# Expert gates of a PEER layer: two tokens interleaved instead of four, and the sum of both parts kept in the order of the activations

## The chip, the cores and the metric

The kernel runs on one core of one Trainium2 chip. The metric is the device time of one execution in microseconds (us): the median of several runs, here three. One further execution was recorded by the hardware profiler, and all rows below are from it. TensorE (PE) multiplies a moving operand by weights that it loads first (PEld), VectorE (DVE) and ScalarE (ACT) work elementwise, SyncE (SP) issues the transfers.

## The reference, cut to what matters

The program is two transformer blocks behind each other on 256 tokens of width 1024. The change lies in the last layer only, a PEER layer: each token picks, in each of 8 heads, 16 of 128 x 128 experts, with a softmax gate for each.

```python
q = (xt @ wq).reshape(T, PEER_HEADS, 2, PEER_HALF)
s = jnp.einsum('thpd,hpnd->thpn', q, subkeys).astype(jnp.float32)
top_s, top_i = lax.top_k(s, PEER_TOPK)
...
gates = jax.nn.softmax(best_s, axis=-1)
...
hdn = jax.nn.gelu(jnp.einsum('cd,chkd->chk', xc, uc).astype(jnp.float32), approximate=False) * gc
return jnp.einsum('chk,chkd->cd', hdn.astype(vc.dtype), vc)
```

An expert's number is 128 i1 + i2. A token has 128 slots (8 heads x 16), each with one i1, one i2 and one gate.

## The kernel before, in words

The layer is computed densely. For every i1 (a row r of 128) one 512 KB tile of `pu` and one of `pv` is loaded. In the first pass (the u pass) the tile of `pu` is split into two f32 parts (`whi` by ACT on L124, `wlo` by DVE on L125) and multiplied with all 256 tokens: 24 matmuls of 256 columns into `pu` (`mm3`, L184 to L186). ACT takes the gelu into `H[i2, r, token]` (L1629). In the second pass (the v pass) `H` of two rows is split (`hs`, ACT on L1728, DVE on L1729) and multiplied with the split tile of `pv`: 12 matmuls of 512 columns per row into the four accumulators `pout`. Between the two, each value of `H` has to be multiplied by its gate.

The gates are made by `gates(g, t0)`, once for each half g of the i1 (64 each) and each group of G = 8 tokens: 64 calls. On the partitions stand the token's 128 slots. DVE compares each slot's i2 with the numbers 0 to 127 (`b`, L1662) and each slot's i1 with the 64 numbers of the half (`e`, L1664), in f16, and multiplies `e` by both f16 parts of the gate (`a`, two calls of L1667). For each token one matmul (L1673) with `b` as weights and `a` as moving operand (2 parts x 64 columns) sums over the slots, so `pw[i2, token, part, i1]` holds the gates of the token twice over, as two parts. ACT copies part 1 out of PSUM to `s` (L1675), DVE adds part 0 (L1676) and multiplies the sum into `H` (L1677).

In memory `b`, `e` and `a` hold four tokens side by side (the last dimension is 4, in blocks n), so that a matmul that picks one token reads its columns 4 elements of f16 apart, which is 8 bytes. `iob` is the list of numbers, each four times. `s` is in the order token, i1, while `H` is in the order i1, token; so L1677 reads `s` with neighbouring elements 64 f32, 256 bytes, apart.

The order is written out by hand: `work()` is a generator, and after every two rows `step()` takes as many pieces from it as its budget allows and as their due rows ask for (`GCOST` and `BUDGET` are constants of the program that the change does not touch). The engines run their instructions in this order. Buffers: `b`, `a` and `pw` have two each, `e` and `s` one.

Of the kernel before, what the change touches and what calls it, by code (L numbers as in the profile page):

```python
# [20 lines left out]
F32 = mybir.dt.float32  # L21
F32R = mybir.dt.float32r
BF16 = mybir.dt.bfloat16
F16 = mybir.dt.float16
I32 = mybir.dt.int32
U32 = mybir.dt.uint32
AF = mybir.ActivationFunctionType
OP = mybir.AluOpType
# [3 lines left out]
P = 128  # L32
# [53 lines left out]
class K:  # L86
# [1515 lines left out]
    def peer(self, out, parked_x):  # L1602
        nc, tc, d = self.nc, self.tc, self.d

        AT = (0, 64, 128)
        G = 8
        with ExitStack() as ctx:
            pool = lambda n, b, **kw: ctx.enter_context(tc.tile_pool(name=self.name(n), bufs=b, reuse_waits="tile", **kw))
            self.pw = pool("ppw", 2, space=PSUM)
# [4 lines left out]
            wk = pool("pwk", 2)  # L1614
            i1b = keep.tile([P, S], F16, name="i1b")
            i2b = keep.tile([P, S], F16, name="i2b")
            g2 = keep.tile([P, 2, S], F16, name="g2")
            iob = keep.tile([P, P, 4], F16, name="iob")
# [34 lines left out]

            def gates(g, t0):

                n, r0 = G // 4, AT[g]
                nr = AT[g + 1] - r0
                t4 = lambda a: a[:, t0:t0 + G].rearrange("p (n t) -> p n t", t=4)
                b = wk.tile([P, n, P, 4], F16, name=self.name("b"), tag="b")
                e = wk.tile([P, n, 64, 4], F16, name=self.name("e"), tag="e", bufs=1)[:, :, :nr]  # L1660
                a = wk.tile([P, n, 2, 64, 4], F16, name=self.name("a"), tag="a")[:, :, :, :nr]
                nc.vector.tensor_tensor(b, t4(i2b).unsqueeze(2).to_broadcast([P, n, P, 4]),  # L1662
                                        iob.unsqueeze(1).to_broadcast([P, n, P, 4]), op=OP.is_equal)
                nc.vector.tensor_tensor(e, t4(i1b).unsqueeze(2).to_broadcast([P, n, nr, 4]),  # L1664
                                        iob[:, r0:r0 + nr].unsqueeze(1).to_broadcast([P, n, nr, 4]), op=OP.is_equal)
                for k in range(2):
                    nc.vector.tensor_tensor(a[:, :, k], t4(g2[:, k]).unsqueeze(2).to_broadcast([P, n, nr, 4]), e, op=OP.mult)  # L1667
                hv = H[:, r0:r0 + nr, t0:t0 + G]
                if TWO[g]:

                    pw = self.pw.tile([P, G, 2, 64], F32, name=self.name("pw"), tag="pw")[:, :, :, :nr]
                    for t in range(G):
                        nc.tensor.matmul(pw[:, t], b[:, t // 4, :, t % 4], a[:, t // 4, :, :, t % 4], start=True, stop=True)  # L1673
                    s = wk.tile([P, G, 64], F32, name=self.name("s"), tag="s", bufs=1)[:, :, :nr]
                    nc.scalar.activation(s, pw[:, :, 1], AF.Copy)  # L1675
                    nc.vector.tensor_tensor(s, pw[:, :, 0], s, op=OP.add)  # L1676
                    nc.vector.tensor_tensor(hv, s.rearrange("p t a -> p a t"), hv, op=OP.mult)  # L1677
                    return
                pw = self.pw.tile([P, G, 64], F32, name=self.name("pw"), tag="pw")[:, :, :nr]
                for t in range(G):  # L1680
                    for k in range(2):
                        nc.tensor.matmul(pw[:, t], b[:, t // 4, :, t % 4], a[:, t // 4, k, :, t % 4], start=k == 0, stop=k == 1)
                nc.vector.tensor_tensor(hv, pw.rearrange("p t a -> p a t"), hv, op=OP.mult)

            def work():

                for c in self.route(keep, sc, room, iob, g2, i1b, i2b):
                    yield ROUTED, c
                for g in range(len(AT) - 1):
                    for t0 in range(0, S, G):  # L1690
                        yield P - 1 + AT[g], GCOST[0] + (GCOST[1] + TWO[g] * GCOST[2]) * (AT[g + 1] - AT[g]) / 64
                        gates(g, t0)

            beside = work()
            due, spare, part = None, 0.0, 0
# [46 lines left out]
            g = H[:, 8:12].rearrange("p a b -> p (a b)")  # L1742
# [44 lines left out]
def _plan(start, stop):  # L1787
# [41 lines left out]
    for n, f in ((1, lambda: ffn(0, 1)), (2, nsa), (3, lambda: (ffn(0, 2), ffn(1, 1))), (4, diff),  # L1829
                 (5, lambda: ffn(1, 2)), (6, block2), (99, peer)):  # L1830
        if start < n <= stop:
            f()
# [172 lines left out]
```

## Time and profile before

| what | us |
|---|---|
| runs | 2250.28, 2257.81, 2260.03 |
| median | 2257.81 |
| profiled execution, its own time | 2247.26 |
| its span, first to last instruction | 2245.6 |

The profiled execution's time is 1.7 us more than its span, and 10.6 us (0.5%) under the median of the runs. The rows tell times within its span. A busy share is that of an engine in a stretch; the chain of work that ended last is followed back from the last instruction and tells which engine's work the end waited for.

### The profile page before, as it was taken

How to read it: one execution, taken by the hardware profiler on the slowest of the kernel's cores; microseconds unless marked ns; L12 is line 12 of the kernel's file. 1: busy time of each engine (PE TensorE's matmuls, PEld its weight loads, DVE VectorE, ACT ScalarE, POOL GpSimd, SP SyncE). 2: the span in 40 equal slices, each digit the busy share in tenths (PEclk: the TensorE clock that was granted, in tenths of full speed). 3: DMA queues.
4: the chain of work that ended last, by engine and by line, in shares of the span. 5: the costliest groups of instructions: out<-in, count | busy, mean ns of one | idle time of the engine just before them, and what ended most of it. 6: DMA issues, size and time to landing. Idle time of an engine off the chain costs nothing.

```text
span 2245.6 us, 34963 instructions
## 1 busy us (share of the span) xinstructions
PE 2195.1 (98%) x13218; PEld 1859.4 (83%) x13218; DVE 1701.5 (76%) x3367; ACT 1172.1 (52%) x1853; POOL 33.3 (1%) x75
## 2 busy tenths in 40 slices
PE   8999999999999998999999999999999999999999
PEld 7887646887788775888787777999999998888887
DVE  6867677997787586786577567898578888997555
ACT  6655575554555564655455444545444445454443
POOL 1000000000000002000000000000000000000000
PEclk9999999999999997999999999999999999999999
DMA  6555415888655441555442125445544445445554
GB/s 217 201 193 166 160 67 188 296 285 266 229 181 186 160 154 66 174 191 189 134 143 85 58 94 188 149 166 192 187 164 158 152 159 194 162 160 177 190 195 150
DMA packets 107561, 383.28 MB, mean 171 GB/s; under 512 B 13440, under 2 KB 13824, under 8 KB 107392
## 3 DMA queue, kind: packets, MB, share of 16 engines
q1 hardware_dynamic: 103392, 374.39, 48.7%
q10 hardware_dynamic: 3360, 4.55, 0.6%
q8 instruction: 104, 1.70, 0.3%
q0 software_dynamic: 640, 2.11, 0.3%
q14 instruction: 65, 0.53, 0.1%
HBM read 378.89 MB, written 2.11 MB: 170 GB/s over the span
## 4 chain that ended last, share of the span: by engine, by line
PE 86%; DVE 8%; ACT 2%; DMA 1%; issue 1%; POOL 1%; ACTq 0%; SPq 0%; DVEq 0%
PE pair L192 13%; PE pair L193 7%; PE pout L186 5%; PE pout L185 5%; PE pout L184 5%; PE pu L184 5%; PE pu L185 5%; PE pu L186 5%; PE bank L184 4%; PE bank L185 4%; PE bank L186 4%; PE pair L184 4%; PE pair L186 4%; PE pair L185 4%; DVE wlo L125 3%; PE pw L1673 3%
## 5 line engine op out<-in xcount | busy, mean ns | idle before, releaser
L124 ACT ACTIVATE whi<-raw 128x1024 fp32r<-128x1024 f32 x654 | 690.9, 1059 | 719.1 <-PE pout L185 141.8
L125 DVE TENSOR_TENSOR wlo<-raw,whi 128x1024 fp32r<-128x1024 f32 x654 | 797.5, 1222 | 288.0 <-ACT whi L124 279.4
L192 PE MATMUL pair<-xx,whi 128*128 128x512 f32 x1280 | 447.6, 395 | 0.0
L193 PE MATMUL pair<-xx,wlo 128*128 128x256 f32 x1280 | 358.0, 280 | 0.3 <-DVE wlo L125 0.3
L184 PE MATMUL pu<-xx,whi 128*128 128x256 f32 x1024 | 292.9, 286 | 1.1 <-ACT H L1629 1.1
L185 PE MATMUL pu<-xx,wlo 128*128 128x256 f32 x1024 | 289.9, 283 | 0.0
L186 PE MATMUL pu<-xx,whi 128*128 128x256 f32 x1024 | 289.7, 283 | 0.0
L192 PEld LDWEIGHTS pair<-xx,whi 128*128 128x128 f32 x1280 | 240.6, 188 | 55.1 <-issue 0.2
L193 PEld LDWEIGHTS pair<-xx,wlo 128*128 128x128 f32 x1280 | 241.9, 189 | 1.1 <-DVE wlo L125 0.7
L184 PE MATMUL pout<-whi,hs 128*128 128x512 f32 x512 | 201.7, 395 | 0.2 <-ACT hs L1728 0.2
L185 PE MATMUL pout<-whi,hs 128*128 128x512 f32 x512 | 199.5, 390 | 0.1
L186 PE MATMUL pout<-wlo,hs 128*128 128x512 f32 x512 | 199.5, 390 | 0.0
L184 PEld LDWEIGHTS pu<-xx,whi 128*128 128x128 f32 x1024 | 196.8, 192 | 1.4 <-ACT H L1629 1.3
L185 PEld LDWEIGHTS pu<-xx,wlo 128*128 128x128 f32 x1024 | 196.5, 192 | 0.0
L186 PEld LDWEIGHTS pu<-xx,whi 128*128 128x128 f32 x1024 | 196.3, 192 | 0.0
L184 PE MATMUL pair<-whi,hT 128*128 128x512 f32 x352 | 138.7, 394 | 6.7 <-DVE x L351 6.7
L186 PE MATMUL pair<-wlo,hT 128*128 128x512 f32 x352 | 139.7, 397 | 0.0
L185 PE MATMUL pair<-whi,lT 128*128 128x512 f32 x352 | 138.6, 394 | 0.0
L184 PE MATMUL bank<-whi,xx 128*128 128x512 f32 x288 | 117.9, 410 | 0.5 <-DVE rsg L168 0.5
L185 PE MATMUL bank<-whi,xx 128*128 128x512 f32 x288 | 115.6, 401 | 0.0
L186 PE MATMUL bank<-wlo,xx 128*128 128x512 f32 x288 | 114.9, 400 | 0.0
L186 PEld LDWEIGHTS pout<-wlo,hs 128*128 128x128 f32 x512 | 96.1, 188 | 20.3
(564 smaller groups left out, 3583.6 us busy)
## 6 DMA issues: line engine op xcount, KB each, us to landing
raw<-in_pu_dram SPq DMA_DIRECT2D x128, 512.0 KB, 3.5
raw<-in_pv_dram SPq DMA_DIRECT2D x128, 512.0 KB, 3.5
raw<-in_f1i_dram SPq DMA_DIRECT2D x88, 512.0 KB, 4.3
raw<-in_f2i_dram SPq DMA_DIRECT2D x88, 512.0 KB, 4.1
araw<-in_wada_dram SPq DMA_DIRECT2D x48, 512.0 KB, 4.6
raw<-in_f1o_dram SPq DMA_DIRECT2D x44, 512.0 KB, 3.5
raw<-in_f2o_dram SPq DMA_DIRECT2D x44, 512.0 KB, 4.1
raw<-in_wi_dram SPq DMA_DIRECT2D x28, 512.0 KB, 3.5
```

The lines of the kernel that those rows point to most:

```text
L124: nc.scalar.activation(hi, raw, AF.Copy)
L125: nc.vector.tensor_tensor(lo, raw, hi.bitcast(F32), op=OP.subtract)
L184: mm(out, lh, rh, start=start, stop=False)
L185: mm(out, ll, rh, start=False, stop=False)
L186: mm(out, lh, rl, start=False, stop=stop)
L192: mm(out, lh, rr, start=start, stop=False)
L193: mm(out[:, 0], ll, rr[:, 0], start=False, stop=stop)
L1673: nc.tensor.matmul(pw[:, t], b[:, t // 4, :, t % 4], a[:, t // 4, :, :, t % 4], start=True, stop=True)
```

## The change

`G` stays 8. The tokens stand in four blocks of two instead of two blocks of four (`Q = 2`), so that one token's columns in `b` and `a` are 2 elements, 4 bytes, apart. Of `iob` only the first two of each four equal numbers are read. `s` is now stored in the order i1, token, as `H` is. So ACT's copy and DVE's add read `pw` in that order: neighbouring elements of their reads of PSUM are 128 f32, 512 bytes, apart, where before they came in runs of 64 neighbours. L1677 reads `s` in one run. The number of instructions and their sizes are the same. The branch for `TWO[g]` false isn't used (`TWO = (True, True)`).

```diff
+        Q = 2
...
-                n, r0 = G // 4, AT[g]
+                n, r0 = G // Q, AT[g]
...
-                b = wk.tile([P, n, P, 4], F16, name=self.name("b"), tag="b")
-                e = wk.tile([P, n, 64, 4], F16, name=self.name("e"), tag="e", bufs=1)[:, :, :nr]
-                a = wk.tile([P, n, 2, 64, 4], F16, name=self.name("a"), tag="a")[:, :, :, :nr]
-                nc.vector.tensor_tensor(b, t4(i2b).unsqueeze(2).to_broadcast([P, n, P, 4]),
-                                        iob.unsqueeze(1).to_broadcast([P, n, P, 4]), op=OP.is_equal)
+                b = wk.tile([P, n, P, Q], F16, name=self.name("b"), tag="b")
+                e = wk.tile([P, n, 64, Q], F16, name=self.name("e"), tag="e", bufs=1)[:, :, :nr]
+                a = wk.tile([P, n, 2, 64, Q], F16, name=self.name("a"), tag="a")[:, :, :, :nr]
+                nc.vector.tensor_tensor(b, tq(i2b).unsqueeze(2).to_broadcast([P, n, P, Q]),
+                                        iob[:, :, :Q].unsqueeze(1).to_broadcast([P, n, P, Q]), op=OP.is_equal)
...
-                        nc.tensor.matmul(pw[:, t], b[:, t // 4, :, t % 4], a[:, t // 4, :, :, t % 4], start=True, stop=True)
-                    s = wk.tile([P, G, 64], F32, name=self.name("s"), tag="s", bufs=1)[:, :, :nr]
-                    nc.scalar.activation(s, pw[:, :, 1], AF.Copy)
-                    nc.vector.tensor_tensor(s, pw[:, :, 0], s, op=OP.add)
-                    nc.vector.tensor_tensor(hv, s.rearrange("p t a -> p a t"), hv, op=OP.mult)
+                        nc.tensor.matmul(pw[:, t], b[:, t // Q, :, t % Q], a[:, t // Q, :, :, t % Q], start=True, stop=True)
+                    s = wk.tile([P, 64, G], F32, name=self.name("s"), tag="s", bufs=1)[:, :nr]
+                    part = pw.rearrange("p t k a -> p k a t")
+                    nc.scalar.activation(s, part[:, 1], AF.Copy)
+                    nc.vector.tensor_tensor(s, part[:, 0], s, op=OP.add)
+                    nc.vector.tensor_tensor(hv, s, hv, op=OP.mult)
```

`e` and `a` are computed as before, with `tq` for `t4` and `Q` for 4.

## Rows read from the trace of the kernel before

**Rows 1.** Busy time by stretch: u pass with gates, v pass with gates, without.

```profile
core 0: us, PE busy (x) PEld busy (x) DVE busy (x) ACT busy (x) POOL busy (x), PEclk, DMA share, GB/s
1655.00:1862.00 207.00, 207.00 (x1734) 205.36 (x1733) 176.73 (x254) 95.55 (x124) 0.00 (x0) 1.00 0.46 157
1862.00:2052.00 190.00, 189.62 (x950) 155.45 (x948) 185.48 (x273) 97.40 (x123) 0.00 (x0) 1.00 0.50 171
2052.00:2221.00 169.00, 169.00 (x747) 139.99 (x746) 95.74 (x95) 82.42 (x94) 0.00 (x0) 1.00 0.55 192
```

**Rows 2.** Chain of work that ended last, 1655 to 2052, by line.

```profile
by line: PE pu L185 14.9%; PE pu L184 14.9%; PE pu L186 14.9%; PE pw L1673 14.6%; PE pout L185 13.5%; PE pout L186 13.4%; PE pout L184 13.2%; DVE wlo L125 0.3%; issue 0.2%; DVE hs L1729 0.2%; DVE b L1662 0.0%
```

**Rows 3.** Pieces of that chain, one step of the v pass: start, us, what.

```profile
1925.94 0.95 PE pw L1673 x8
1926.90 0.24 PE pout L184
```

**Rows 4.** Timeline of TensorE: start, length, first u pass, then v pass.

```profile
1701.00 0.28 PE L185 MATMUL pu<-xx,wlo 128*128 128x256 f32 x1
...
1701.95 0.28 PE L184 MATMUL pu<-xx,whi 128*128 128x256 f32 x1
...
1927.21 0.39 PE L186 MATMUL pout<-wlo,hs 128*128 128x512 f32 x1
...
1931.97 0.39 PE L186 MATMUL pout<-wlo,hs 128*128 128x512 f32 x1
```

**Rows 5.** Timeline of the weight loads behind 16 matmuls of one column.

```profile
434.74 1.87 PEld L898 LDWEIGHTS bank<-ones,acc 128*128 128x128 f32 x16
436.52 0.19 PEld L192 LDWEIGHTS pair<-xx,whi 128*128 128x128 f32 x1
```

**Rows 6.** Groups of weight loads: busy us, mean ns of one, idle before.

```profile
L1673 PEld LDWEIGHTS <-b 128*128 128x128 f16 x512 | 52.5, 118 | 9.3 <-DVE wlo L125 4.2 <-issue 2.3 <-DVE e L1664 0.5
L898 PEld LDWEIGHTS bank<-ones,acc 128*128 128x128 f32 x64 | 7.5, 192 | 0.4 <-ACT R L419 0.2
```

**Rows 7.** Groups of VectorE, 1862 to 2052.

```profile
L125 DVE TENSOR_TENSOR wlo<-raw,whi 128x1024 fp32r<-128x1024 f32 x59 | 72.2, 1224 | 1.8 <-PE pw L1673 1.5 <-ACT whi L124 0.3
L1677 DVE TENSOR_TENSOR H<-s,H 128x512 f32<-128x512 f32 x31 | 34.2, 1102 | 0.0
L1667 DVE TENSOR_TENSOR a<-g,e 128x512 f16<-128x512 f16 x60 | 24.7, 422 | 0.0
L1729 DVE TENSOR_TENSOR hs<-H,hs 128x512 fp32r<-128x512 f32 x32 | 22.1, 692 | 0.0
L1676 DVE TENSOR_TENSOR s<-pw,s 128x512 f32<-128x512 f32 x32 | 22.0, 687 | 0.0
L1662 DVE TENSOR_TENSOR b<-i2b,iob 128x1024 f16<-128x1024 f16 x30 | 20.8, 692 | 4.3 <-PE pw L1673 4.2
L1664 DVE TENSOR_TENSOR e<-i1b,iob 128x512 f16<-128x512 f16 x29 | 12.3, 424 | 0.0
```

**Rows 8.** Groups of VectorE, whole span: writes by steps (L555), short runs (L1406).

```profile
L555 DVE TENSOR_TENSOR X<-bank,cpos 64x512 f32<-64x512 f32 x4 | 4.5, 1115 | 0.1
L555 DVE TENSOR_TENSOR X<-bank,cpos 64x448 f32<-64x448 f32 x4 | 3.9, 982 | 0.1
L1406 DVE TENSOR_TENSOR rt<-mqk,cos 128x64 f32<-128x64 f32 x4 | 0.9, 222 | 0.0
```

**Rows 9.** Groups of ScalarE, 1655 to 2052.

```profile
L124 ACT ACTIVATE whi<-raw 128x1024 fp32r<-128x1024 f32 x120 | 127.5, 1062 | 202.1 <-issue 89.7 <-PE pu L186 61.4 <-PE pout L185 51.0
L1675 ACT ACTIVATE s<-pw 128x512 f32<-128x512 f32 x63 | 37.3, 593 | 2.0
```

**Rows 10.** Timeline of one v step: the copy, and VectorE up to the add.

```profile
1926.93 0.60 ACT L1675 ACTIVATE s<-pw 128x512 f32<-128x512 f32 x1
...
1927.54 1.22 DVE L125 TENSOR_TENSOR wlo<-raw,whi 128x1024 fp32r<-128x1024 f32 x1
...
1928.68 0.68 DVE L1676 TENSOR_TENSOR s<-pw,s 128x512 f32<-128x512 f32 x1
```

**Rows 11.** Waits, 1862 to 2052: us in total, times, longest.

```profile
DVE b L1662 <- PE pw L1673: 4.2, 13, 1.5
PEld L1673 <- DVE wlo L125: 4.2, 16, 0.3
```

More of the change, by code (lines that the diff above doesn't have):

```diff
@@ L1654, in gates @@
             def gates(g, t0):
-                n, r0 = G // 4, AT[g]
+                n, r0 = G // Q, AT[g]
                 nr = AT[g + 1] - r0
-                t4 = lambda a: a[:, t0:t0 + G].rearrange("p (n t) -> p n t", t=4)
-                b = wk.tile([P, n, P, 4], F16, name=self.name("b"), tag="b")
-                e = wk.tile([P, n, 64, 4], F16, name=self.name("e"), tag="e", bufs=1)[:, :, :nr]
-                a = wk.tile([P, n, 2, 64, 4], F16, name=self.name("a"), tag="a")[:, :, :, :nr]
-                nc.vector.tensor_tensor(b, t4(i2b).unsqueeze(2).to_broadcast([P, n, P, 4]),
-                                        iob.unsqueeze(1).to_broadcast([P, n, P, 4]), op=OP.is_equal)
-                nc.vector.tensor_tensor(e, t4(i1b).unsqueeze(2).to_broadcast([P, n, nr, 4]),
-                                        iob[:, r0:r0 + nr].unsqueeze(1).to_broadcast([P, n, nr, 4]), op=OP.is_equal)
+                tq = lambda a: a[:, t0:t0 + G].rearrange("p (n t) -> p n t", t=Q)
+                b = wk.tile([P, n, P, Q], F16, name=self.name("b"), tag="b")
[3 more added lines that the diff above has]
+                                        iob[:, :, :Q].unsqueeze(1).to_broadcast([P, n, P, Q]), op=OP.is_equal)
+                nc.vector.tensor_tensor(e, tq(i1b).unsqueeze(2).to_broadcast([P, n, nr, Q]),
+                                        iob[:, r0:r0 + nr, :Q].unsqueeze(1).to_broadcast([P, n, nr, Q]), op=OP.is_equal)
                 for k in range(2):
-                    nc.vector.tensor_tensor(a[:, :, k], t4(g2[:, k]).unsqueeze(2).to_broadcast([P, n, nr, 4]), e, op=OP.mult)
+                    nc.vector.tensor_tensor(a[:, :, k], tq(g2[:, k]).unsqueeze(2).to_broadcast([P, n, nr, Q]), e, op=OP.mult)
                 hv = H[:, r0:r0 + nr, t0:t0 + G]
@@ L1681, in gates @@
                     for k in range(2):
-                        nc.tensor.matmul(pw[:, t], b[:, t // 4, :, t % 4], a[:, t // 4, k, :, t % 4], start=k == 0, stop=k == 1)
+                        nc.tensor.matmul(pw[:, t], b[:, t // Q, :, t % Q], a[:, t // Q, k, :, t % Q], start=k == 0, stop=k == 1)
                 nc.vector.tensor_tensor(hv, pw.rearrange("p t a -> p a t"), hv, op=OP.mult)
```

## The prediction

> **What bounds the kernel now.** I read the busy times by stretch first, to find what is full where the change acts [rows 1]. The 64 calls of `gates` run between about 1655 and 2052 us, 32 in the u pass and 32 in the v pass. The reader should see two things. TensorE is busy throughout (207.0 of 207.0 us, 189.6 of 190.0) at a granted clock of 1.00, the upper level, 2.4 GHz. And VectorE, with 176.7 of 207 us in the u pass, is nearly as full in the v pass: 185.5 of 190. ScalarE is half idle. The chain of work then says which of the two the end waits for [rows 2]: TensorE nearly everywhere, and L1673, the gates' matmul, alone has 14.6% of the stretch. A call's eight matmuls take 0.95 us of that chain [rows 3], 0.119 us each. The waits agree [rows 11]: in the v pass VectorE waits 4.2 us for L1673 to give back a buffer, so it is a little ahead of TensorE, and the weight loads of L1673 wait 4.2 us for VectorE. The two are nearly in balance there. So a saving on TensorE counts at once in the u pass, and in the v pass as far as VectorE can follow; a saving on VectorE alone gives almost nothing; and VectorE has (190 - 185.5) / 32 = 0.14 us a call to lose in the v pass before it sets the pace.
>
> **The matmuls (columns 4 bytes apart, not 8).** No row shows an f16 matmul at another step, so I bound it. The f32 matmuls read columns that are 4 bytes apart, as the new operands are. In the u pass 8 of them go from 1701.00 to 1701.95, 0.119 us for 256 columns; in the v pass 21 go from 1927.21 to 1931.97, 0.227 us for 512 [rows 4]. That is 0.108 us per 256 columns and 0.011 us for each matmul. By these rows 128 columns would take 0.054 + 0.011 = 0.065 us; L1673 takes 0.119, as if its columns came at half that rate. Its weight load could be the reason too. Sixteen f32 loads behind matmuls of one column start 1.78 / 16 = 0.111 us apart [rows 5], and the record of such a load is 0.192 us long, so 0.081 us of a record do not hold up the next load. The f16 load's record is 0.118 us [rows 6], which leaves 0.037 us. If that is hidden behind the matmul in front, a pair takes 0.065 us; if it stands in series, 0.102; if the step has nothing to do with it, 0.119. I take 0.084, the middle of the first two, since the rows of equal step speak for one of them and nothing tells which. A call then saves 8 x 0.035 = 0.28 us, at least 0 and at most 8 x 0.054 = 0.43.
>
> The Trainium skill has a rule that speaks against this ("SBUF — State Buffer", Specifications (TRN2)): SBUF is read in lines of 16 bytes, and two accesses to a line are enough for full bandwidth. At 8 bytes the old step already had two. By that rule nothing is saved on TensorE, and the time would be that of the first rival below; by the f32 rows it is 0.28 us a call.
>
> **VectorE's last pass, L1677.** It takes 1.10 us for 512 elements, where the passes of L1676 and L1729 with the same size take 0.69 [rows 7]. Its `s` operand is read 256 bytes apart. Another pass that goes by large steps, L555, shows the same: from 448 to 512 elements it grows by 133 ns, 2.1 ns an element, whereas f32 passes in one run grow from 0.687 to 1.224 us over 512 elements, 1.05 ns [rows 7, 8]. `H` itself is read and written in runs of 8; L1406, with runs of 8 on one side, takes 0.222 us for 64 elements, and 0.687 - 448 x 0.00105 = 0.217 is what one run would take. So the step of `s` is the cause, and I take 0.69 us for L1677: 0.41 saved a call; the other end is no saving.
>
> **The reads of PSUM, L1676 and L1675.** Now these go by large steps, 512 bytes. No row reads PSUM so. Below: nothing, 0.69 and 0.59 us as now. Above: as L1677 does in SBUF, 1.10 us for the add, and 0.59 + 512 x 0.00092 = 1.06 us for the copy (ACT's row of 1024 elements less that of 512 is 0.47 us, 0.00092 an element) [rows 7, 9]. The copy is covered: ScalarE is half idle, and in the v step it is done at 1927.53 while the add starts at 1928.68, behind a pass of `wlo` and more [rows 10]; 0.47 us later still comes before it. Without that cover VectorE would stand still before the add, and `a`, `b` and `wlo` behind it. For the add I take no cost, with little confidence (nearer by shape is L1677, nearer by memory are L1676 as it is and every other read of PSUM), and keep 0.41 for the range.
>
> The skill's page "PSUM — Partial Sum Buffer" (Specifications (TRN2)) has lines of 8 bytes there and warns of patterns that are not contiguous, for matmuls. Were VectorE's reads meant too, the add would take back what L1677 saves, and the time would be the 2246 us below.
>
> **The compares and products, L1662, L1664, L1667.** Their f16 passes run at twice the rate of f32: 0.692 us for 1024 elements where `wlo` takes 1.224 [rows 7]. Rows of operands are now 2 elements long, and `iob` has a gap after each pair. I take no cost, since two neighbours are still there to be taken together; the other end is that all four fall to the f32 rate: 0.53 + 0.26 + 2 x 0.26 = 1.31 us a call.
>
> **The sum.** U pass: TensorE saves 32 x 0.28 = 9.0 us, and VectorE's 176.7 - 13.1 us fit easily in 198. V pass: TensorE comes to 190 - 9.0 = 181 us, VectorE to 185.5 - 32 x 0.41 = 172.4, so the 9.0 count too. Together 18 us. The profiled execution goes from 2247.3 to 2229.3 us; it lies 10.6 us under the median of the runs, and I put the same saving on that median: 2257.8 - 18 = 2240 us. If the add takes the 0.41 us back, VectorE needs its 185.5 us in the v pass, which then can't fall below about 186.5: 9.0 + 3.5 = 12.5, 2245 to 2246 us. With pairs of 0.065 us and a free add it is 64 x 0.43 = 27.5 us, 2230.
>
> **Rivals.** *The step doesn't matter to TensorE.* The pair stays at 0.119 us, held by loading weights or something else of fixed length. For it: the weight load's record is just as long as the pair, 0.118 us [rows 6]. Against it: f32 loads have longer records and yet pairs as short [rows 4, 6]. VectorE's saving then falls into its own idle time; the v pass could lose the few small waits of its weight loads: 0 to 3 us, 2255 to 2258.
>
> *VectorE loses the double rate.* If the pairs of two stop the f16 passes from taking two at a time, a call costs 1.31 - 0.41 = 0.90 us more. In the v pass VectorE needs 185.5 + 28.8 = 214 us, 24 over the 190. In the u pass it needs 176.7 + 28.8 = 205.5, just within the 207, so that TensorE's saving there is eaten. 2257.8 + 24 = 2282 us, slower by 1.1%. It decides as soon as a call costs VectorE 0.14 us more in the v pass. For it: only rows of 4 elements have been seen at this rate. Against it: the rate needs two neighbours, and there are two.
>
> *The add gets dearer and L1677 no cheaper*, if it is `H` and not `s` that holds it: 0.41 us more a call, 185.5 + 13.1 = 198.6 us in the v pass, 9 us over; with TensorE's saving in the u pass about 2258, without it 2266.
>
> **How the numbers follow.** TensorE's pairs get shorter and VectorE is no worse than now: 0.53 (0.33 with a cheap add, around 2240; 0.20 with a dear one, around 2246). The pair stays: 0.29, 2256. The double rate lost: 0.08, 2282. Dear add and old L1677: 0.10, 2258 to 2266. I predict the likeliest, 2240 us, its own range 2230 to 2247. The range of 2230 to 2264 leaves out the lost double rate and small pieces at both ends, together under 2 in 10. A change under 0.5%, 11.3 us, is about what a measurement of this kernel can't tell from none. Faster by more needs the first case: nearly all of its cheap add and over half of its dear one, 0.46. Slower by more: the lost rate and a part of the last rival, 0.13. The rest, 0.41, is the same.
>
> **What would show it.** In the profile after, eight matmuls of L1673 should take 0.67 us of the chain instead of 0.95 (0.52 if the load is hidden; 0.95 means the first rival). L1677 should read 0.69 us; L1676 0.69 and L1675 0.59, or 1.10 and 1.06 at the other end; L1662 0.69, L1664 and L1667 0.42, or 1.22 and 0.69 if the double rate is lost. VectorE's busy time in the v pass should fall by some 13 us. The prediction is wrong if L1673 keeps its 0.95 us, or if TensorE's matmuls turn up waiting for VectorE in the v pass.

## The result, and the profile after

| | before | after |
|---|---|---|
| median of the runs, us | 2255.53 (4 runs, 2250.28 to 2260.03) | 2231.39 (4 runs, 2227.63 to 2232.28) |
| profiled execution, its own time, us | 2247.26 | 2232.00 |
| its span, us | 2245.6 | 2230.3 |

The ratio is 0.9891, 95% interval 0.9864 to 0.9917: the change saves 24.1 us, 1.1%. The forecast was 2240 us, in a range of 2230 to 2264, from the 2257.81 us of three runs; the median before is now that of four.

In the new kernel `b` stands on L1663, `e` on L1665, `a` on L1668, the gates' matmul on L1674, the copy on L1677, the add on L1678, the product with `H` on L1679, and `hs` on L1730 and L1731: each one or two lines further down than before.

I cut both traces at the same events: the first matmul of the gates, the first of the v pass, the last of the gates, and the end. First the kernel before, busy time of each engine by stretch:

```profile
1652.10:1863.00 210.90, 210.65 (x1763) 208.68 (x1761) 179.46 (x256) 98.58 (x129) 0.00 (x0) 1.00 0.46 158
1863.00:2050.50 187.50, 187.37 (x937) 153.75 (x937) 183.22 (x270) 95.59 (x120) 0.00 (x0) 1.00 0.49 169
2050.50:2245.60 195.10, 190.66 (x843) 157.60 (x840) 108.37 (x109) 87.48 (x100) 0.00 (x0) 1.00 0.52 181
```

The same three stretches of the kernel after:

```profile
core 0: us, PE busy (x) PEld busy (x) DVE busy (x) ACT busy (x) POOL busy (x), PEclk, DMA share, GB/s
1663.50:1860.80 197.30, 196.13 (x1762) 194.67 (x1760) 168.10 (x256) 98.36 (x129) 0.00 (x0) 1.00 0.51 169
1860.80:2035.20 174.40, 174.35 (x935) 141.14 (x936) 171.12 (x270) 92.03 (x120) 0.00 (x0) 1.00 0.56 182
2035.20:2230.30 195.10, 190.71 (x844) 157.59 (x841) 108.01 (x109) 87.82 (x100) 0.00 (x0) 0.99 0.55 181
```

The u pass is 13.6 us shorter (210.9 to 197.3), the v pass 13.1 (187.5 to 174.4), the rest is 195.1 us both times. So the change took 26.7 us out of the stretch in which it acts, and nothing behind it. TensorE is still busy with hardly a gap in both passes (196.1 of 197.3 us, 174.35 of 174.40). VectorE has 11.4 us less to do in the u pass and 12.1 in the v pass, and is as nearly full there as before, 171.1 of 174.4 us. The spans differ by only 15.3 us because the profiled execution of the new kernel came to the gates 11.4 us later (1663.5 against 1652.1). That has nothing to do with the change: up to the gates the program is the same. In the profiled executions of the seven kernels below, where this holds too, the first matmul of the gates starts anywhere from 1656.5 to 1668.2 us. In these two most of the lag goes with the granted clock of an earlier part. Between 200 and 400 us, before and then after:

```profile
200.00:400.00 200.00, 188.74 (x1003) 127.46 (x1004) 146.35 (x494) 124.87 (x306) 2.77 (x10) 0.98 0.43 144
...
200.00:400.00 200.00, 187.21 (x942) 120.92 (x941) 138.05 (x477) 119.12 (x298) 2.77 (x10) 0.92 0.39 129
```

The clock was 0.98 in the one and 0.92 in the other, and 1003 matmuls against 942 got done. That the medians differ by 24.1 us, near the 26.7 of the stretch, shows that most of the 11.4 us belongs to those two executions.

The chain of work that ended last, 1655 to 2052, by line, answers to [rows 2]; below it pieces of a u step, answering to [rows 3]:

```profile
by line: PE pu L184 16.1%; PE pu L186 15.7%; PE pu L185 15.7%; PE pout L184 15.3%; PE pout L186 14.7%; PE pout L185 14.7%; PE pw L1674 7.4%; ACT whi L124 0.3%; ACT hs L1730 0.1%; ACT H L1630 0.1%; issue 0.0%
...
1701.72 0.12 PE pu L186
1701.83 0.47 PE pw L1674 x8
1702.31 0.17 PE pu L184
```

Eight matmuls of the gates take 0.47 us of the chain, 0.058 each, where it was 0.95 and 0.119; their share of the chain falls from 14.6% to 7.4%. Over all 64 calls that is 64 x 0.48 = 30.7 us less, and 26.7 of it reached the end of the stretch. Most of the rest is taken back by the first f32 matmul behind each call: it takes 0.17 us in the piece above, where the other matmuls of the u pass take 0.12, and in the v pass 0.29 us, where it was 0.24 [rows 3]. The distance from one call to the next shows what is left. Two neighbouring calls of the u pass and two of the v pass, in the kernel before:

```profile
1659.92 0.95 PE pw L1673 x8
...
1666.62 0.95 PE pw L1673 x8
...
2043.37 0.95 PE pw L1673 x8
...
2049.79 0.95 PE pw L1673 x8
```

The same in the kernel after:

```profile
1676.71 0.47 PE pw L1674 x8
...
1682.99 0.47 PE pw L1674 x8
...
2022.95 0.47 PE pw L1674 x8
...
2028.95 0.47 PE pw L1674 x8
2029.42 0.29 PE pout L184
```

From call to call it is 6.28 us instead of 6.70 in the u pass, and 6.00 instead of 6.42 in the v pass. So a call saves 0.42 us in the end, and 64 x 0.42 = 26.9 us is nearly all that the stretch lost. What makes the f32 matmul behind a call longer was not tested.

The groups of VectorE from 1862 to 2052, answering to [rows 7]:

```profile
L125 DVE TENSOR_TENSOR wlo<-raw,whi 128x1024 fp32r<-128x1024 f32 x63 | 76.9, 1221 | 7.7 <-ACT whi L124 7.4
L1668 DVE TENSOR_TENSOR a<-g,e 128x512 f16<-128x512 f16 x60 | 24.5, 417 | 0.0
L1731 DVE TENSOR_TENSOR hs<-H,hs 128x512 fp32r<-128x512 f32 x34 | 23.2, 685 | 0.0
L1679 DVE TENSOR_TENSOR H<-s,H 128x512 f32<-128x512 f32 x32 | 21.9, 684 | 0.0
L1678 DVE TENSOR_TENSOR s<-pw,s 128x512 f32<-128x512 f32 x32 | 21.9, 683 | 0.0
L1663 DVE TENSOR_TENSOR b<-i2b,iob 128x1024 f16<-128x1024 f16 x29 | 19.9, 687 | 1.2 <-PE pw L1674 0.2
L1665 DVE TENSOR_TENSOR e<-i1b,iob 128x512 f16<-128x512 f16 x29 | 12.1, 418 | 0.0
```

Only one row has moved: the product with `H`, from 1102 to 684 ns. The add, which now reads PSUM 512 bytes apart, has 683 (687 before); the f16 passes on pairs of tokens have 687, 418 and 417 (692, 424, 422). ScalarE's copy out of PSUM, answering to [rows 9], and the gates' weight loads, answering to [rows 6]:

```profile
L1677 ACT ACTIVATE s<-pw 128x512 f32<-128x512 f32 x64 | 37.4, 584 | 0.0
...
L1674 PEld LDWEIGHTS <-b 128*128 128x128 f16 x512 | 29.4, 97 | 8.6 <-DVE e L1665 3.4 <-issue 1.8 <-DVE a L1668 1.3
```

The copy has 584 ns (593 before). The record of a weight load, which was as long as a pair of load and matmul (118 and 119 ns), is now far longer than the pair: 97 against 58 ns. So the record of such a load is not a time that TensorE has to spend in full on each pair. Three of the waits of the v pass, 1859 to 2036, answering to [rows 11] (us in total, times, longest):

```profile
PEld L1674 <- DVE e L1665: 3.4, 13, 0.3
...
DVE b L1663 <- PE pw L1674: 1.3, 2, 1.0
PE pout L184 <- ACT hs L1730: 1.2, 1, 1.2
```

VectorE now waits only twice for TensorE, and the first matmul of the v pass waits 1.2 us for the first `hs`. Otherwise TensorE's matmuls do not wait: they fill 174.35 of the 174.40 us.

### The profile page after: what moved, and what is told of

Same layout as the page of the kernel before. It is cut to its first block, busy times and chain, and to the rows that moved or that the text cites. A ratio compares the mean times of both kernels' runs of the same rounds, so it can differ in the third digit from the quotient of the medians.

```text
span 2230.3 us, 34963 instructions
## 1 busy us (share of the span) xinstructions
PE 2180.0 (98%) x13218; PEld 1839.1 (82%) x13218; DVE 1678.6 (75%) x3367; ACT 1168.9 (52%) x1853; POOL 33.3 (1%) x75
## 4 chain that ended last, share of the span: by engine, by line
PE 86%; DVE 8%; DMA 2%; ACT 2%; issue 1%; POOL 1%; SPq 0%; ACTq 0%; DVEq 0%
PE pair L192 13%; PE pair L193 7%; PE pout L184 5%; PE pout L185 5%; PE pout L186 5%; PE pu L184 5%; PE pu L185 5%; PE pu L186 5%; PE bank L184 4%; PE bank L185 4%; PE bank L186 4%; PE pair L184 4%; PE pair L185 4%; PE pair L186 4%; DVE wlo L125 3%; PE pw L1674 1%
```

## The experiments

The change has three parts that could have saved the time: the step between the columns of `a` (the moving operand), the step in `b` (the weights, loaded anew for each matmul), and the new order of the sum, which relieves VectorE. The theory was that the moving operand alone decides: TensorE takes in its columns at full rate when they are 4 bytes apart and at half that rate at 8. One rival was that loading the weights got faster, another that the sum's part brings the gain. Each experiment starts from the kernel after.

**Only the weights at 4 bytes** (`b` in twos, `a` and `e` in fours).

```diff
-        Q = 2
+        Q, QB = 4, 2
...
-nc.tensor.matmul(pw[:, t], b[:, t // Q, :, t % Q], a[:, t // Q, :, :, t % Q], ...)
+nc.tensor.matmul(pw[:, t], b[:, t // QB, :, t % QB], a[:, t // Q, :, :, t % Q], ...)
```

> The changed kernel, but with the moving operand (a, e) four tokens interleaved again, 8 bytes between columns; the weights (b) stay at 4 bytes. Theory M (the moving operand's columns come at half rate at 8 bytes): a call's eight matmuls take 0.95 us of the chain again, as before, and the time is that of before, 2250 to 2258. Theory W (the weight load reads at half rate): 0.47 us, 2231 as with the whole change. Both in part: between 0.55 and 0.85 us.

Measured: 2256.5 us (10 runs) against 2256.3 before (20 runs), ratio 1.0014 (0.9988 to 1.0039). A piece of the chain:

```profile
1677.66 0.94 PE pw L1674 x8
```

The eight matmuls are back at 0.94 us and the whole gain is gone, although the weights are read at the small step and the sum has its new order. So neither of these is the cause by itself.

**Only the moving operand at 4 bytes** (`a` and `e` in twos, `b` in fours).

```diff
-        Q = 2
+        Q, QB = 2, 4
```

The rest as in the experiment above.

> The reverse: the moving operand (a, e) at 4 bytes between columns, the weights (b) at 8 again. Theory M: eight matmuls take 0.47 us and the time is 2231. Theory W: 0.95 us and 2250 to 2258. Both in part: between 0.55 and 0.85 us.

Measured: 2232.06 us (4 runs), ratio 0.9912 (0.9878 to 0.9947). Two pieces of the chain, the eight matmuls:

```profile
1679.90 0.50 PE pw L1674 x8
...
1686.21 0.51 PE pw L1674 x8
```

Nearly all of the gain is there. 0.50 against 0.47 us says that the step of the weights is worth some 0.03 to 0.04 us a call, 64 x 0.035 = 2 us, too little for the runs to tell.

**Only the new sum** (operands in fours).

```diff
-        Q = 2
+        Q = 4
```

> Only the second half of the change: four tokens interleaved everywhere as before, the sum kept in the order i1, token. My theory (TensorE sets the pace in both passes): VectorE's pass over H reads 0.69 us, its busy time in the v pass falls by 13 us, eight matmuls stay at 0.95 us, and the time is 0 to 3 us under before, 2252 to 2256. Rival (VectorE's saving counts by itself in the v pass, where it was 98% busy): 8 to 13 us less, 2243 to 2247.

Measured: 2255.1 us (10 runs), ratio 0.9996 (0.9973 to 1.0019). A piece of the chain, the group of the product with `H`, and the v pass:

```profile
1681.95 0.95 PE pw L1674 x8
...
L1679 DVE TENSOR_TENSOR H<-s,H 128x512 f32<-128x512 f32 x31 | 21.2, 685 | 0.0
...
1871.60:2059.00 187.40, 187.25 (x935) 153.60 (x936) 173.26 (x270) 95.27 (x120) 0.00 (x0) 1.00 0.52 169
```

VectorE's product is 0.42 us shorter in each call, 13 us over the pass, but its busy time there falls by only 9.9 us, from 183.2 to 173.3. (Its passes overlap, and the time in which two run is counted once. Added up one by one they take 14.0 us less; but they overlap less, too.) The pass takes 187.4 us, as before (187.5), because TensorE sets its length. Those 9.9 us of VectorE's time are worth nothing here that the runs can tell.

**Only the operands** (in twos, the sum in its old order).

```diff
-                    s = wk.tile([P, 64, G], F32, ...)[:, :nr]
-                    part = pw.rearrange("p t k a -> p k a t")
-                    nc.scalar.activation(s, part[:, 1], AF.Copy)
-                    nc.vector.tensor_tensor(s, part[:, 0], s, op=OP.add)
-                    nc.vector.tensor_tensor(hv, s, hv, op=OP.mult)
+                    s = wk.tile([P, G, 64], F32, ...)[:, :, :nr]
+                    nc.scalar.activation(s, pw[:, :, 1], AF.Copy)
+                    nc.vector.tensor_tensor(s, pw[:, :, 0], s, op=OP.add)
+                    nc.vector.tensor_tensor(hv, s.rearrange("p t a -> p a t"), hv, op=OP.mult)
```

> Only the first half of the change: two tokens interleaved, the sum in the order token, i1 as before. My theory: eight matmuls take 0.47 us; in the u pass all of it counts, 32 x 0.48 = 15 us; in the v pass TensorE would need 190 - 15 = 175 us, VectorE still its 185 (its pass over H stays at 1.10 us), so VectorE becomes the bound there, with TensorE's matmuls waiting for it, and 3 to 5 us are saved: 18 to 20 us under before, 2236, some 5 to 10 us over the whole change. Rival (the order of the sum gives nothing): 2231, as the whole change.

Measured: 2234.12 us (5 runs, 2227.6 to 2240.8), ratio 0.9908 (0.9877 to 0.9939). Here the product with `H` is on L1678. Its group in the v pass, the busy times of that pass, and a wait in it:

```profile
L1678 DVE TENSOR_TENSOR H<-s,H 128x512 f32<-128x512 f32 x30 | 32.5, 1083 | 0.0
...
1865.50:2044.00 178.50, 174.92 (x935) 141.09 (x936) 178.50 (x268) 92.75 (x120) 0.00 (x0) 1.00 0.53 174
...
PEld L1674 <- DVE a L1668: 6.2, 9, 2.3
```

VectorE is busy for 178.5 of 178.5 us and TensorE's weight loads wait up to 2.3 us for `a`: the bound of the v pass has passed to VectorE, as expected. But the pass saves 9.0 us (187.5 to 178.5) and not the 3 to 5 of the theory, which counted on VectorE's old 185 us. In the profiles this costs 178.5 - 174.4 = 4.1 us against the kernel after. In the medians it is 2.7 us, less than the 5 to 10 expected and less than the runs can tell: the intervals of the two ratios overlap. So the second part of the change is worth up to some 4 us, and only because the first part made TensorE faster.

**One token to a block** (columns 2 bytes apart).

```diff
-        Q = 2
+        Q = 1
```

> The changed kernel with one token a block (Q = 1): columns of both operands 2 bytes apart, and VectorE's compares and products have no two neighbours to take together. My theory: eight matmuls stay at 0.47 us (the column rate is reached at 4 bytes already); b reads 1.22 us, e and a 0.69 us each, 1.31 us more a call than the changed kernel; VectorE becomes the bound in the v pass (about 168 + 42 = 210 us there in place of 174), and in the u pass it is just full; the time is that of the second rival, 2265 to 2282. Rival (TensorE gains again from contiguous columns, or VectorE keeps its double rate): eight matmuls under 0.44 us, or b at 0.69 us and 2231.

Measured: 2282.83 us (4 runs) against 2256.04 before (7 runs), ratio 1.0127 (1.0106 to 1.0147): slower. The eight matmuls in the chain, and the f16 passes of VectorE from 1862 to 2088:

```profile
1681.39 0.46 PE pw L1674 x8
...
L1668 DVE TENSOR_TENSOR a<-g,e 128x512 f16<-128x512 f16 x64 | 42.0, 686 | 0.0
L1663 DVE TENSOR_TENSOR b<-i2b,iob 128x1024 f16<-128x1024 f16 x31 | 37.8, 1219 | 0.0
L1665 DVE TENSOR_TENSOR e<-i1b,iob 128x512 f16<-128x512 f16 x31 | 21.3, 686 | 0.0
```

TensorE gains nothing from 2 bytes over 4 (0.46 against 0.47 us), and the f16 passes fall to the f32 rate: 1219 and 686 ns instead of 687 and 418. The busy times of the u pass and of the v pass, then 30 us within the v pass, and the wait that leads there:

```profile
1660.60:1861.40 200.80, 196.51 (x1746) 193.79 (x1744) 198.58 (x247) 100.19 (x128) 0.00 (x0) 1.00 0.50 163
1861.40:2087.40 226.00, 196.09 (x966) 152.47 (x967) 217.53 (x280) 97.17 (x122) 0.00 (x0) 0.94 0.44 146
...
2010.00:2040.00 30.00, 23.86 (x125) 18.76 (x123) 29.98 (x40) 12.10 (x17) 0.00 (x0) 0.89 0.36 123
...
PEld L1674 <- DVE a L1668: 31.1, 25, 3.7
```

VectorE sets the pace: 217.5 of 226 us in the v pass, with waits of TensorE's loads of 31.1 us together. That is the price of the second rival of the prediction, had its condition been met: it gave 2282 us.

**`a` and `e` with all eight tokens in a block** (16 bytes apart, `b` in fours). `e` and `a` are computed through views of 2 x 4 tokens.

```diff
-        Q = 2
+        Q, QB = 8, 4
...
-                    nc.vector.tensor_tensor(a[:, :, k], tq(g2[:, k])..., e, op=OP.mult)
+                    nc.vector.tensor_tensor(by4(a[:, 0, k]), h4(g2[:, k]), by4(e[:, 0]), op=OP.mult)
```

> The sum in the new order, weights at 8 bytes as before, the moving operand eight tokens interleaved: 16 bytes between columns. Theory P (beyond 4 bytes a column the moving operand's rate falls in proportion to the bytes that its columns span): 128 columns take four times 0.053 us, eight matmuls some 1.75 us of the chain, 64 x 0.80 = 51 us more than before, about 2305. Theory S (two speeds, full and half): 0.95 us and 2250 to 2258.

Measured: 2315.29 us in one run. In this kernel the matmul is on L1675; a piece of the chain:

```profile
1676.97 1.85 PE pw L1675 x8
```

It is 0.231 us a pair, 0.90 us a call more than at 8 bytes. 64 x 0.90 = 58 us, and the run is 59 us over the median before, 2256.04. That is theory P (1.75 us, about 2305) and a little more; theory S is out.

**`a` padded to three f16** (6 bytes apart). With one buffer of `a` instead of two; its time, 2248.65 us in one run, is not compared for that reason, only the matmuls are.

```diff
-                a = wk.tile([P, n, 2, 64, Q], F16, ..., tag="a")[:, :, :, :nr]
+                a = wk.tile([P, n, 2, 64, 3], F16, ..., tag="a", bufs=1)[:, :, :, :nr, :Q]
```

> The changed kernel with each pair of tokens in a padded to three, 6 bytes between the moving operand's columns, and one buffer of a in place of two, for want of room; so its time is not compared, only the matmuls inside a call. Theory P: 128 columns take 1.5 times 0.053 us, a pair 0.085, eight 0.68 us. Theory S: 0.95 us, or 0.47 if half speed begins only at 8 bytes.

Measured, in the chain:

```profile
1685.05 0.71 PE pw L1674 x8
```

It is 0.089 us a pair, midway between 0.058 at 4 bytes and 0.118 at 8. Theory P gave 0.68 us for the eight, theory S 0.95 or 0.47. (It is 0.71 or 0.72 us in 53 of the chain's 62 pieces of this kind; the others, most of them right behind a wait for `a`, have 0.84 to 0.86.)

The seven kernels and the two of the case give one table, for f16 columns of the moving operand, 128 of them to a matmul:

| bytes from column to column | 8 matmuls, us | one, us | from |
|---|---|---|---|
| 2 | 0.46 | 0.057 | one token to a block |
| 4 | 0.47 | 0.058 | after, operands only (0.50 with the weights at 8 bytes) |
| 6 | 0.71 | 0.089 | padded |
| 8 | 0.94 to 0.95 | 0.118 | before, weights only, sum only |
| 16 | 1.85 | 0.231 | all eight tokens |

From 2 to 4 bytes the step costs nothing. Beyond, the time follows the bytes spanned: 0.71, 0.95 and 1.85 are 1.5, 2.0 and 3.9 times 0.47.

## Why the prediction held, step by step

**What bounds the kernel.** Right. TensorE set the end in both passes; the sum alone, which frees VectorE, changed nothing; and the saving on TensorE counted in both passes, 13.6 and 13.1 us.

**The matmuls.** The mechanism was right: columns of f16 at 8 bytes came at half the rate of those at 4. The size was off, and this is the mis-sized term: the 0.037 us for a part of the load that does not fit behind the matmul in front, half of which I took. With it a pair was put at 0.084 us, and a call was to save 0.28 us. The pair measures 0.058 in the chain, and a call saves 0.42 us by the distance from call to call. That is nearly the 0.43 us of the other end, the f32 rate with 0.011 us of fixed time for each matmul and the load hidden. That end was right for what a call costs, but not in its parts: the pairs are shorter than its 0.065 us, by nearly as much as the f32 matmul behind them is longer, and that it comes out so close may be chance. The load's record is no price: at 97 ns it is longer than the pair that holds it.

The rule of the Trainium skill that I set against it ("SBUF — State Buffer", Specifications (TRN2)), two accesses to a line of 16 bytes are enough, does not hold for TensorE's moving operand as I read it. By it 8 bytes would be as good as 4; the runs have 0.95 against 0.47 us. The page says more exactly that at least two are needed, and that each cross to a new line has a price; but a step of 2 bytes, which crosses half as often as one of 4, gains nothing here (0.46 against 0.47 us).

**The product with `H`.** Right: 0.69 us forecast, 0.684 measured, and with the old order of `s` still 1.083. So it was the step of `s`, not `H`.

**The reads of PSUM.** Right, though taken with little confidence: the add has 0.683 us and the copy 0.584, at steps of 512 bytes. The warning of the Trainium skill about patterns that are not contiguous ("PSUM — Partial Sum Buffer", Specifications (TRN2)) is meant for matmuls there, and the trace shows no such cost for reads by VectorE and ScalarE. The dear end, 1.10 us, is out, and with it the last rival, a dearer add beside an unchanged product.

**The compares and products.** Right: rows of two keep the double rate (687, 418 and 417 ns). Rows of one lose it (1219, 686 and 686 ns).

**The sum.** 18 us forecast, from 9.0 in each pass; 26.7 measured in the profile and 24.1 in the medians. The difference is what a call saves: 64 x 0.43 = 27.5 us, named as the end with pairs of 0.065 us, was nearly what came. One more piece was too large: without a cheaper product VectorE was to need the 185.5 us that it had in the stretch of the v pass. By the cut used here that is 183.2 us in 270 passes; with the old sum and the new operands it finished the pass in 178.5, in 268. One pass of `wlo` and one product fewer are 2.3 us. The other 2.4 us are passes that are each a little shorter (the product 1083 ns against 1102) and overlap a little more. So here the busy time of an engine that waits now and then was more than it needed when it set the pace.

**The rivals.** The one in which the step does not matter fell: L1674 has 0.47 us, not 0.95. The lost double rate did not come with two tokens; with one it came, at the price that was worked out: 2282 us forecast, 2282.83 measured. The working of that number was less good than its sum. By the cut used here it put the v pass at 187.5 + 24 = 211.5 us, and it has 226; it let the u pass stay at 210.9, and that has 200.8. In the u pass VectorE was busy for 198.6 us, but with 247 passes instead of 256: the compares and products of two calls, and one `wlo`, were left to the v pass, which has 280 instead of 270. By the means of their groups those nine passes take 7.9 us; with them the u pass would come to some 206 us, near the 205.5 forecast. So most of the 10 us that the u pass seems to keep of TensorE's saving was moved into the v pass, where TensorE waited for VectorE up to 3.7 us at a time. The errors in the two passes, +14.5 and -10.1, nearly cancel, and in the main for this reason; that the sum is right to 1 us is luck all the same.

## What to carry to other kernels

When f16 operands are interleaved so that VectorE can work at its double rate, interleave no more than it needs: two tokens kept that rate, and the columns of the moving operand 4 bytes apart kept TensorE at its own, while four cost half of it. Put the strided access where it is free: here reads of PSUM at 512 bytes cost VectorE and ScalarE nothing, while a read of SBUF at 256 bytes cost VectorE 0.4 us on top of 0.7. Before you count on a saving, read which engine sets the length of the stretch: the same cheaper product on VectorE was worth nothing that could be measured before TensorE got faster, and up to some 4 us afterwards.

## What the hardware showed beside it

The step of the moving operand is not a matter of two rates. From 4 to 16 bytes the matmul's time grows in proportion to the bytes that its columns span, at 6 bytes too. The step of the weights hardly counts: 0.03 to 0.04 us for eight loads between 4 and 8 bytes, and nothing where the moving operand is at 8 (0.94 and 0.95 us).

In the kernel with one token to a block the granted clock of the v pass is 0.94 in the mean and 0.89 in the 30 us shown above, where TensorE is busy for 23.9 of 30 us and its loads wait for VectorE; in the same pass of the other kernels, where TensorE has few gaps, it is 0.99 or 1.00, the upper level, 2.4 GHz. Whether the lower clock made that pass longer, in which VectorE sets the pace, was not separated.
